# The memory's rows split in the attention, and the mixers' four 8 KB slots kept through the cross attention

## The chip, the cores and the metric

The kernel runs on one core of a Trainium2 chip. The metric is device microseconds of one execution, the median of several runs. Every row of a trace below comes from one execution that the hardware profiler recorded.

## What is computed

One decoder layer on a sequence of 512 tokens of width 1024, in four sub-layers with residual adds, each behind an RMS norm: half a SwiGLU feed-forward layer (inner width 2816), two parallel mixers (a spatial gating unit and a causal dilated window attention), a cross attention of four heads to 256 fixed memory rows, and another half feed-forward layer. What the change touches lies in the second and third:

```python
y_a = chunked_spatial_gating(z_sgu, sgu_ln_g[l], sgu_ln_b[l], sgu_w_s[l], sgu_b_s[l])
y_b = dilated_mixture_attention(q, k, v).reshape(b, s, D_ATT)
y = jnp.concatenate([rmsnorm(y_a, out_norm_a[l]), rmsnorm(y_b, out_norm_b[l])], axis=-1)
x = x + y @ w_out[l]

h = rmsnorm(x, cross_norm[l])
m = rmsnorm(mem, mem_norm[l])
x = x + memory_cross_attention(h, m, cross_wq[l], cross_wk[l], cross_wv[l], cross_wo[l])
```

## The kernel before

Everything is kept transposed, as eight tiles `X[d]` of 128 channels by 512 tokens in SBUF. Every product is made as three matmuls of a shortened format: each operand is split into a high part and a low part (`split`, L103 on ScalarE for the high part and L104 on VectorE for the low part, the source less the high part), and `mm3` (L127 to L129) adds high x high, high x low and low x high in PSUM. In the trace L129 is the matmul that needs a weight's low part, `wlo`, and L127 and L128 need `whi` only.

Weights pass through `load_weight` (L116): a raw tile `wraw` by DMA from SyncE's queue (SP), then the split into `whi` and `wlo`. The raw, high and low tiles have three slots each, so the weights of a fourth matrix tile are split when the first one's matmuls are done.

PSUM has four banks for long sums (`acc`) and four for short ones (`aux`).

The kernel is written against a framework with a planner. It orders each engine's instructions ahead of time, by their place in the program and a cost model, lets a later instruction go first when an earlier one isn't ready by the model, gives out the slots of a pool's tag in that order and sets the semaphores. On the chip each engine then works through its own list in that order.

The stages around the change, in the order of the program:

- `mixers`: a pool `mix` holds U, V and the normalised V as high and low part (`vnH`, `vnL`), four tiles of 8 KB per partition under the tag `t8`. `z_block` makes the five blocks of the input projection. Then come 32 units of the window attention, (m, r, i) for four head pairs, two heads and four tiles of 128 queries: `scores(u)` makes the score row and its softmax, `transposes(u - 3)` turns the probabilities, `values(u - 4)` multiplies them with v and writes `yH`, `yL` for inner tile 4 + m. `qk_transpose(1)`, ahead of unit 12, turns the q and k of the second two head pairs out of the tiles `qk` and splits them (`qkH`, `qkL`).
- At the end of `mixers` the sum of squares of the attention's output becomes `Rb`: `Stats.column` (L186), eleven short VectorE steps (`rsqrt_cols`, L134 to L143), `dg` (L151), one matmul (L153), one copy (`R`, L157).
- `cross` opens a pool of its own where `mix` lay, and calls `mem_split` first. It loads the memory's 1024 x 256 values in four transfers of two tiles (`mraw`, L664, two slots), scales each tile by its gain and the memory's norm (L666), and splits them into `mH`, `mL`, in eight slots of the pool of 512-wide tiles `hp`.
- `mix_out` is the output projection. Part 0 takes the four inner tiles of the gating unit, part 1 the four of the attention, each for d = 0 to 7 with twelve matmuls. Part 0 adds its sum to X (L627). Part 1 multiplies it with `Rb` (`yo`, L630), adds it to X (L631), and splits X for the next norm (`hH` L202, `hL` L203), with its square (L178), which GpSimd adds up (L170).
- Then the value projection of the memory (`xvH`, `xvL`, four tiles of 4 KB), the key projection, the queries, scores and values of four heads with `xpt` (four slots of 4 KB), and the output projection.

Of the kernel before, what the change touches and what calls it, by code (L numbers as in the profile page):

```python
# [17 lines left out]
F32 = mybir.dt.float32  # L18
F32R = mybir.dt.float32r
I32 = mybir.dt.int32  # L20
AF = mybir.ActivationFunctionType
ALU = mybir.AluOpType
AX = mybir.AxisListType

P = 128
S = 512
D = 1024
KD = D // P
# [4 lines left out]
NM = 256  # L33
NT = S // P
# [12 lines left out]
G_FFN1, G_MIX, G_CROSS, G_MEM, G_FFN2, G_FIN, G_OA, G_OB, G_BS = (  # L47
    0, 8, 16, 24, 32, 40, 48, 52, 56)
# [6 lines left out]
def body(tc, I, out):  # L55
    nc = tc.nc
    from contextlib import ExitStack
    ctx = ExitStack()
    with ctx:
# [27 lines left out]
        def gcol(off, k):  # L87
            return gains[:, off + k:off + k + 1]
# [4 lines left out]
        def aux_tile():  # L93
            return paux.tile([P, S], F32, name="aux", tag="aux")

        def h_tile(n):
            return hp.tile([P, S], F32R, name=n, tag="h")

        def f32(ap):
            return ap.bitcast(F32)  # L100

        def split(hi, lo, src):
            ins = nc.scalar.activation(hi, src, AF.Copy)  # L103
            nc.vector.tensor_sub(lo, src, f32(hi))  # L104
            return ins
# [280 lines left out]
        def h_sl(h, k, ts):  # L386
            return h[0][k][:, ts], h[1][k][:, ts]

        def mixers(norm, cs):
            col = []  # L390
            hshape = [P, 8, 64]
            with tc.tile_pool(name="mix", bufs=1) as mp:
# [12 lines left out]
                split(ws[0], ws[1], wsr)  # L405


                U = mp.tile([P, NT, S], F32, name="U", tag="t8", bufs=4)
                V = mp.tile([P, NT, S], F32, name="V", tag="t8", bufs=4)

                def gelu_to(dst):
                    def evac(t, acc):
                        nc.scalar.activation(dst[:, t], acc, AF.Gelu, scale=col[0][:, t:t + 1])
                    return evac

                z_block(norm, 0, gelu_to(U), lambda: col.append(norm.stats.column(D)))
                z_block(norm, 1, gelu_to(V))

                qk = {}
# [18 lines left out]
                def qk_transpose(b):  # L438
                    for m in range(4):
                        ps = aux_tile()  # L440
                        for t in range(NT):
                            nc.tensor.transpose(ps[:, t * P:(t + 1) * P],
                                                qk[t][:, m * P:(m + 1) * P], ident_b)
                        if m >= 2:
                            hi, lo = h_tile("qkH"), h_tile("qkL")
                            split(hi, lo, ps)
                            kT[2 * b + m % 2] = (hi, lo)
                            continue


                        qT[2 * b + m % 2] = []
                        for r in range(2):
                            hi, lo = h_tile("qkH"), h_tile("qkL")
                            rows, other = (slice(x * 64, (x + 1) * 64) for x in (r, 1 - r))
                            for x in (hi, lo):
                                nc.gpsimd.memset(f32(x[other]), 0.0)
                            split(hi[rows], lo[rows], ps[rows])
                            qT[2 * b + m % 2].append((hi, lo))

                vH = [h_tile("vH") for _ in range(NT)]  # L460
                vL = [h_tile("vL") for _ in range(NT)]

                def v_evac(t, acc):
# [9 lines left out]

                mu = mp.tile([P, NT, 8], F32, name="mu")
                var = mp.tile([P, NT, 8], F32, name="var")
                vn = (mp.tile([P, NT, S], F32R, name="vnH", tag="t8", bufs=4),
                      mp.tile([P, NT, S], F32R, name="vnL", tag="t8", bufs=4))
                for t in range(NT):
                    vt = V[:, t].rearrange("p (g c) -> p g c", g=8)
                    nc.vector.tensor_reduce(mu[:, t], vt, axis=AX.X, op=ALU.add)  # L480
                    nc.vector.tensor_scalar(mu[:, t], mu[:, t], 1.0 / 64, None, op0=ALU.mult)
                    nc.vector.tensor_sub(vt, vt, mu[:, t, :, None].to_broadcast(hshape))
                    sq = mp.tile([P, S], F32, name="vsq", tag="s2", bufs=SB)
                    nc.scalar.activation(sq, V[:, t], AF.Square)
                    nc.vector.tensor_reduce(var[:, t], sq.rearrange("p (g c) -> p g c", g=8),
                                            axis=AX.X, op=ALU.add)
                rs = rsqrt_cols(var.rearrange("p t g -> p (t g)"), NT * 8, 1.0 / 64, LN_EPS, "lnr")
                for t in range(NT):
                    vt = V[:, t].rearrange("p (g c) -> p g c", g=8)
                    r = rs[:, t * 8:(t + 1) * 8]  # L490
                    nc.vector.tensor_mul(vt, vt, r[:, :, None].to_broadcast(hshape))
                    nc.vector.tensor_mul(V[:, t], V[:, t], lng)
                    nc.vector.tensor_add(V[:, t], V[:, t], lnb)
                    split(vn[0][:, t], vn[1][:, t], V[:, t])
# [72 lines left out]
                def gate_mix():  # L567

                    for g in range(0, 8, 2):
                        ps = aux_tile().rearrange("p (a t c) -> p a t c", a=2, t=NT)  # L570
                        for a in range(2):
                            cs_ = slice((g + a) * 64, (g + a + 1) * 64)
                            mm3(ps[:, a], ws, (vn[0][:, :, cs_], vn[1][:, :, cs_]),
                                (slice(None), g + a), slice(None), True, True)
                            nc.vector.scalar_tensor_tensor(U[:, :, cs_], ps[:, a],
                                                           gcol(G_BS, g + a), U[:, :, cs_],
                                                           op0=ALU.add, op1=ALU.mult)
                    ssa = mp.tile([P, NT], F32, name="ssa")
                    for t in range(NT):
                        sq = mp.tile([P, S], F32, name="usq", tag="s2", bufs=SB)  # L580
                        nc.scalar.activation(sq, U[:, t], AF.Square, accum_out=ssa[:, t:t + 1])
                    ra = rsqrt_cols(ssa, NT, 1.0 / S, NORM_EPS, "ra4")
                    for t in range(NT):
                        nc.scalar.activation(U[:, t], U[:, t], AF.Copy, scale=ra[:, t:t + 1])

                yH, yL = [None] * KD, [None] * KD

                def gate_out():
                    for b in range(4):
                        ps = aux_tile()  # L590
                        for t in range(NT):
                            nc.tensor.transpose(ps[:, t * P:(t + 1) * P],
                                                U[:, t, b * P:(b + 1) * P], ident)
                        yH[b], yL[b] = h_tile("yH"), h_tile("yL")
# [5 lines left out]
                nu = len(units)  # L600
# [5 lines left out]
                for u in range(LAG, nu + LAG + 1):  # L606
                    if u == nu // 2 - LAG - 1:
                        qk_transpose(1)
                    if u < nu:
                        scores(u)  # L610
                    transposes(u - LAG) if u - LAG < nu else None
                    if u > LAG:
                        values(u - LAG - 1)
# [20 lines left out]
        mem = {}  # L634
# [22 lines left out]
            elif step == 4:  # L657
                mem["R"] = rows(mem["col"], 2, "mR")

        def mem_split(pool, mR):  # L660
            mH, mL = [], []
            for k in range(0, KD, 2):
                raw = pool.tile([P, 2, NM], F32, name="mraw", tag="mraw", bufs=2)
                nc.sync.dma_start(raw, I["memT"][k:k + 2].rearrange("k p n -> p k n"))  # L664
                for j in range(2):
                    nc.vector.scalar_tensor_tensor(raw[:, j], raw[:, j], gcol(G_MEM, k + j), mR,  # L666
                                                   op0=ALU.mult, op1=ALU.mult)
                hi = h_tile("mH").rearrange("p (k n) -> p k n", k=2)
                lo = h_tile("mL").rearrange("p (k n) -> p k n", k=2)
                split(hi, lo, raw)  # L670
                mH += [hi[:, 0], hi[:, 1]]
                mL += [lo[:, 0], lo[:, 1]]
            return mH, mL

        def cross(norm, y, mR, nxt):
            with tc.tile_pool(name="cross", bufs=1) as cp:
                m = mem_split(cp, mR)
                mix_out(cp, *y, norm)

                vH = [cp.tile([P, D], F32R, name=f"xvH{t}") for t in range(2)]  # L680
                vL = [cp.tile([P, D], F32R, name=f"xvL{t}") for t in range(2)]
                for blk in range(2):
                    acc = [acc_tile() for _ in range(2)]
                    for kk in range(4):
                        w = load_weight(I["wv"][blk, kk], [2, S])
                        for t in range(2):
                            for k2 in range(2):
                                k = 2 * kk + k2
# [73 lines left out]
                for h in range(4):  # L762
                    scores(h, 0)
                    scores(h, 2)
                    if h < 3:
                        queries(2 * h + 2)
                    pt = tuple(cp.tile([P, 2, S], F32R, name="xpt", tag="xpt", bufs=4)
                               for _ in range(2))
                    transposes(h, 0, pt)
                    transposes(h, 2, pt)  # L770
                    if h < 3:
                        queries(2 * h + 3)
                    values(2 * h, pt)
                    values(2 * h + 1, pt)
# [15 lines left out]
        n1, n2, n3, n4 = (  # L790
            Norm(g, t) for g, t in ((G_FFN1, 1), (G_MIX, 0), (G_CROSS, 0), (G_FFN2, 0)))
# [6 lines left out]
        cs = []  # L798
# [5 lines left out]
                mem_rows(d)  # L804

        ffn(n1, I["gate1"], I["up1"], I["down1"], n2, lambda: w0, between)
        y = mixers(n2, cs[0])
        cross(n3, y, mem["R"], n4)
        ffn(n4, I["gate2"], I["up2"], I["down2"], None)


# [83 lines left out]
```

## Time and profile before

| | |
|---|---|
| median of three runs | 1129.87 us (1128.18 to 1129.97) |
| the profiled execution | 1129.09 us |
| its span | 1127.3 us |
| TensorE busy | 1110.1 us (98%) |
| VectorE busy | 590.9 us (52%) |
| ScalarE busy | 425.0 us (38%) |
| GpSimd busy | 74.3 us (7%) |

The span is the time from the first to the last instruction in the trace; the execution's own time lies 1.8 us above it. Shares of busy time are means over stages that differ much. Matmuls are pipelined, so that their durations overlap: how far apart two of them start says more than how long one is.

### The profile page before, as it was taken

The numbers are of one execution on the slowest core, as the hardware profiler recorded it, in microseconds if no ns is written. First come the engines' busy times: TensorE is split into PE (matmuls) and PEld (weight loads), VectorE is DVE, ScalarE is ACT, GpSimd is POOL, SyncE is SP. The second block draws the span as 40 slices with busy tenths as digits, with TensorE's granted clock in tenths as the row PEclk, the third lists the DMA queues.
The fourth block names the chain that finished last, engine by engine and source line by source line (L and its number), as shares of the span: only waits on it lengthen the run. The fifth ranks groups of instructions, "written<-read, shape, count | busy, mean of one in ns | idle before, by whom it ended". The sixth has DMA issues, their size and how long they took to land. (4 is left out here: it accounts for less than half of the span.)

```text
span 1127.3 us, 13958 instructions
## 1 busy us (share of the span) xinstructions
PE 1110.1 (98%) x5472; PEld 934.7 (83%) x5472; DVE 590.9 (52%) x1027; ACT 425.0 (38%) x672; POOL 74.3 (7%) x98
## 2 busy tenths in 40 slices
PE   9999999999999999999989999999999999999996
PEld 7788888888888888888868988878888888888996
DVE  4544533444444447679796555455444334445542
ACT  6333312233233434568665344333332222333421
POOL 2000100000002200011121000120000000000011
PEclk9999999999999999999999999999999999999998
DMA  6322334222233423110136421222222333223511
GB/s 220 113 94 89 115 89 126 105 94 94 72 92 109 149 90 108 38 48 29 57 118 203 147 75 57 72 97 90 98 93 66 103 113 111 95 94 115 155 64 38
DMA packets 39698, 110.79 MB, mean 98 GB/s; under 512 B 4432, under 2 KB 9296, under 8 KB 39632
## 3 DMA queue, kind: packets, MB, share of 16 engines
q1 hardware_dynamic: 39632, 109.89, 30.3%
q8 instruction: 43, 0.70, 0.2%
q14 instruction: 23, 0.19, 0.1%
HBM read 107.78 MB, written 2.10 MB: 97 GB/s over the span
## 5 line engine op out<-in xcount | busy, mean ns | idle before, releaser
L103 ACT ACTIVATE whi<-wraw 128x1024 fp32r<-128x1024 f32 (+2 forms) x213 | 202.8, 953 | 513.9 <-PE acc L128 298.6
L104 DVE TENSOR_TENSOR wlo<-wraw,whi 128x1024 fp32r<-128x1024 f32 (+2 forms) x213 | 237.0, 1115 | 163.0 <-ACT whi L103 162.7
L127 PE MATMUL acc<-hH,whi 128*128 128x512 f32 x768 | 301.0, 392 | 0.6 <-ACT hH L202 0.6
L128 PE MATMUL acc<-hL,whi 128*128 128x512 f32 x768 | 299.4, 390 | 0.8 <-DVE hL L203 0.8
L129 PE MATMUL acc<-hH,wlo 128*128 128x512 f32 x768 | 299.4, 390 | 0.5 <-DVE wlo L104 0.5
L128 PEld LDWEIGHTS acc<-hL,whi 128*128 128x128 f32 x768 | 144.3, 188 | 31.5 <-DVE hL L203 1.5
L127 PEld LDWEIGHTS acc<-hH,whi 128*128 128x128 f32 x768 | 144.3, 188 | 31.4 <-ACT hH L202 1.0
L129 PEld LDWEIGHTS acc<-hH,wlo 128*128 128x128 f32 x768 | 144.3, 188 | 30.7 <-DVE wlo L104 1.0
L127 PE MATMUL acc<-hidH,whi 128*128 128x512 f32 (+1 forms) x308 | 115.6, 375 | 0.0
L129 PE MATMUL acc<-hidH,wlo 128*128 128x512 f32 (+1 forms) x308 | 115.3, 374 | 0.0
L128 PE MATMUL acc<-hidL,whi 128*128 128x512 f32 (+1 forms) x308 | 115.3, 374 | 0.0
L170 POOL TENSOR_TENSOR sq<-sq 128x512 f32<-128x512 f32 (+1 forms) x39 | 49.2, 1260 | 775.5 <-ACT sq L178 775.1
L247 DVE TENSOR_TENSOR u<-acc,R 128x512 f32<-128x512 f32 x44 | 30.4, 690 | 121.6 <-PE acc L129 121.6
L243 DVE TENSOR_TENSOR gp<-acc,R 128x512 f32<-128x512 f32 x44 | 30.4, 691 | 85.4 <-PE acc L129 81.7
L129 PEld LDWEIGHTS acc<-hidH,wlo 128*128 128x128 f32 x308 | 58.1, 189 | 10.3
L128 PEld LDWEIGHTS acc<-hidL,whi 128*128 128x128 f32 x308 | 58.1, 188 | 10.3
L127 PEld LDWEIGHTS acc<-hidH,whi 128*128 128x128 f32 x308 | 58.1, 189 | 10.2
L127 PE MATMUL acc<-whi,hH 128*128 128x512 f32 x160 | 62.5, 391 | 0.0
L129 PE MATMUL acc<-whi,hL 128*128 128x512 f32 x160 | 62.4, 390 | 0.0
L230 DVE SCALAR_TENSOR_TENSOR x<-acc,x 128x512 f32<-128x512 f32 (+1 forms) x40 | 23.3, 584 | 74.6 <-PE acc L129 74.6
L128 PE MATMUL acc<-wlo,hH 128*128 128x512 f32 x160 | 62.3, 390 | 0.0
L178 ACT ACTIVATE sq<-x 128x512 f32<-128x512 f32 (+1 forms) x48 | 26.1, 551 | 41.5 <-DVE x L230 38.9
(213 smaller groups left out, 1488.1 us busy)
## 6 DMA issues: line engine op xcount, KB each, us to landing
wraw<-up SPq DMA_DIRECT2D x44, 512.0 KB, 3.5
wraw<-gate SPq DMA_DIRECT2D x43, 512.0 KB, 3.5
wraw<-down SPq DMA_DIRECT2D x28, 384.0 KB, 3.1
wraw<-w_in SPq DMA_DIRECT2D x20, 512.0 KB, 3.5
wraw<-down SPq DMA_DIRECT2D x28, 320.0 KB, 2.9
wraw<-w_out SPq DMA_DIRECT2D x16, 256.0 KB, 2.7
wraw<-wv SPq DMA_DIRECT2D x8, 512.0 KB, 3.5
wraw<-wk SPq DMA_DIRECT2D x8, 512.0 KB, 4.2
```

What stands on the lines that cost most here:

```text
L103: ins = nc.scalar.activation(hi, src, AF.Copy)
L104: nc.vector.tensor_sub(lo, src, f32(hi))
L127: nc.tensor.matmul(ps, lhsT=aH, rhs=bH, start=start, stop=False)
L128: nc.tensor.matmul(ps, lhsT=aH, rhs=bL, start=False, stop=False)
L129: nc.tensor.matmul(ps, lhsT=aL, rhs=bH, start=False, stop=stop)
L170: nc.gpsimd.tensor_add(self.parts[0], self.parts[0], sq)
L178: nc.scalar.activation(sq, src, AF.Square)
L230: nc.vector.scalar_tensor_tensor(X[d][:, tok], acc, 0.5, X[d][:, tok], op0=ALU.mult, op1=ALU.add)
L243: nc.vector.tensor_mul(gp, ps[0], R)
L247: nc.vector.tensor_mul(u, ps[1], R)
```

## The change

A pool `big` with the four 8 KB slots of tag `t8` is opened around `mixers` and `cross`. U, V, `vnH`, `vnL` are taken from it as before. `mem_split` moves into the loop of the attention, ahead of unit 16 of 32; its four raw tiles take the four slots of `qk` in the mixers' pool (they had two slots of their own), and its results are two tiles of 8 KB in `big`, not eight of `hp`. In `cross` the memory's values `xvH`, `xvL` become two 8 KB tiles of `big`, and the high and low part of a head's probabilities, `xpt`, share one 8 KB tile of `big`. What is computed stays the same, instruction by instruction.

```diff
-        def mixers(norm, cs):
+        def mem_split(pool, big, mR):
+            mH, mL = (big.tile([P, KD, NM], F32R, name=n, tag="t8", bufs=4) for n in ("mH", "mL"))
+            for k in range(0, KD, 2):
+                raw = pool.tile([P, 2, NM], F32, name="mraw", tag="qk", bufs=4)
+                nc.sync.dma_start(raw, I["memT"][k:k + 2].rearrange("k p n -> p k n"))
+                for j in range(2):
+                    nc.vector.scalar_tensor_tensor(raw[:, j], raw[:, j], gcol(G_MEM, k + j), mR,
+                                                   op0=ALU.mult, op1=ALU.mult)
+                split(mH[:, k:k + 2], mL[:, k:k + 2], raw)
+            return [mH[:, k] for k in range(KD)], [mL[:, k] for k in range(KD)]
+
+        def mixers(norm, cs, big):
...
-                U = mp.tile([P, NT, S], F32, name="U", tag="t8", bufs=4)
-                V = mp.tile([P, NT, S], F32, name="V", tag="t8", bufs=4)
+                U = big.tile([P, NT, S], F32, name="U", tag="t8", bufs=4)
+                V = big.tile([P, NT, S], F32, name="V", tag="t8", bufs=4)
...
                 for u in range(LAG, nu + LAG + 1):
                     if u == nu // 2 - LAG - 1:
                         qk_transpose(1)
+                    if u == nu // 2:
+                        mem["split"] = mem_split(mp, big, mem["R"])
                     if u < nu:
                         scores(u)
...
-        def cross(norm, y, mR, nxt):
+        def cross(norm, y, m, nxt, big):
             with tc.tile_pool(name="cross", bufs=1) as cp:
-                m = mem_split(cp, mR)
                 mix_out(cp, *y, norm)
 
-                vH = [cp.tile([P, D], F32R, name=f"xvH{t}") for t in range(2)]
-                vL = [cp.tile([P, D], F32R, name=f"xvL{t}") for t in range(2)]
+                vH, vL = (big.tile([P, 2, D], F32R, name=n, tag="t8", bufs=4)
+                          for n in ("xvH", "xvL"))
+                vH, vL = ([x[:, t] for t in range(2)] for x in (vH, vL))
...
-                    pt = tuple(cp.tile([P, 2, S], F32R, name="xpt", tag="xpt", bufs=4)
-                               for _ in range(2))
+                    pt = big.tile([P, 2, 2, S], F32R, name="xpt", tag="t8", bufs=4)
+                    pt = tuple(pt[:, i] for i in range(2))
...
-        y = mixers(n2, cs[0])
-        cross(n3, y, mem["R"], n4)
+        with tc.tile_pool(name="big", bufs=1) as big:
+            y = mixers(n2, cs[0], big)
+            cross(n3, y, mem["split"], n4, big)
```

## Rows read from the trace of the kernel before

**Rows 1.** The page's first two parts: busy microseconds of each engine with its share of the span and its instructions; then the span in 40 equal slices of 28 us, a digit being the busy share in tenths.

```profile
PE 1110.1 (98%) x5472; PEld 934.7 (83%) x5472; DVE 590.9 (52%) x1027; ACT 425.0 (38%) x672; POOL 74.3 (7%) x98
...
DVE  4544533444444447679796555455444334445542
```

**Rows 2.** Busy time of each engine by windows of time (from the span's start): the window's length, then busy microseconds and instructions of each engine, then the mean granted clock of TensorE, the busy share of the DMA engines and GB/s.

```profile
510.00:520.00 10.00, 9.95 (x63) 8.24 (x62) 9.63 (x28) 8.61 (x22) 0.48 (x2) 1.00 0.01 2
520.00:530.00 10.00, 10.00 (x68) 8.74 (x66) 9.37 (x32) 7.58 (x22) 1.16 (x6) 1.00 0.16 47
530.00:540.00 10.00, 10.00 (x67) 8.87 (x66) 8.85 (x31) 8.07 (x24) 2.34 (x7) 1.00 0.18 61
540.00:550.00 10.00, 10.00 (x63) 8.25 (x62) 9.57 (x31) 7.90 (x22) 2.01 (x5) 1.00 0.07 27
...
555.00:560.00 5.00, 5.00 (x33) 4.33 (x32) 2.88 (x5) 2.09 (x5) 0.00 (x0) 1.00 0.20 57
...
575.00:580.00 5.00, 1.18 (x5) 0.42 (x4) 5.00 (x7) 2.31 (x4) 2.05 (x2) 1.00 0.00 0
580.00:590.00 10.00, 10.00 (x37) 8.06 (x38) 9.96 (x12) 5.51 (x7) 4.71 (x3) 0.83 0.58 210
```

**Rows 3.** TensorE's matmuls of part 1 of `mix_out` in order of time: start and duration in us, engine, line, output and inputs, and in brackets the idle time before and what ended it.

```profile
558.66 0.40 PE L127 MATMUL acc<-yH,whi 128*128 128x512 f32 x1
...
574.28 0.39 PE L127 MATMUL acc<-yH,whi 128*128 128x512 f32 x1
...
574.96 0.39 PE L128 MATMUL acc<-yL,whi 128*128 128x512 f32 x1
577.09 0.47 PE L127 MATMUL acc<-yH,whi 128*128 128x512 f32 x1 [1.74 <-DVE yo L630]
...
579.88 0.50 PE L129 MATMUL acc<-yH,wlo 128*128 128x512 f32 x1 [2.09 <-DVE wlo L104]
...
581.03 0.63 PE L127 MATMUL acc<-yH,whi 128*128 128x512 f32 x1
581.45 0.63 PE L128 MATMUL acc<-yL,whi 128*128 128x512 f32 x1
...
584.01 0.47 PE L127 MATMUL acc<-yH,whi 128*128 128x512 f32 x1
584.33 0.40 PE L128 MATMUL acc<-yL,whi 128*128 128x512 f32 x1
```

**Rows 4.** Windows again, of two microseconds behind that wait; the third number from the end is the granted clock.

```profile
582.00:584.00 2.00, 2.00 (x6) 1.53 (x5) 2.00 (x5) 1.79 (x3) 0.40 (x1) 0.50 0.31 125
```

**Rows 5.** VectorE in order of time from the rsqrt for `Rb` to the `wlo` that TensorE waits for.

```profile
561.19 0.16 DVE L134 TENSOR_SCALAR rcolbv<-aux 128x4 f32<-128x4 f32 x1 [1.33 <-PE aux L186]
...
562.19 0.16 DVE L141 TENSOR_TENSOR rcolbt<-rcolby 128x4 f32<-128x4 f32 x1
...
565.48 0.87 DVE L151 TENSOR_SCALAR dg<-const,rcolby 128x128 f32<-128x128 f32 x4
...
567.51 0.88 DVE L666 SCALAR_TENSOR_TENSOR mraw<-mraw,gains,R 128x256 f32<-128x256 f32 x2
568.30 0.69 DVE L630 TENSOR_TENSOR yo<-acc,R 128x512 f32<-128x512 f32 x1
568.90 0.48 DVE L666 SCALAR_TENSOR_TENSOR mraw<-mraw,gains,R 128x256 f32<-128x256 f32 x1
569.30 0.68 DVE L104 TENSOR_TENSOR mL<-mraw,mH 128x512 fp32r<-128x512 f32 x1
569.90 0.48 DVE L666 SCALAR_TENSOR_TENSOR mraw<-mraw,gains,R 128x256 f32<-128x256 f32 x1
...
574.56 1.77 DVE L203 SCALAR_TENSOR_TENSOR hL<-x,gains,hH 128x512 fp32r<-128x512 f32 x1
...
579.15 0.68 DVE L104 TENSOR_TENSOR wlo<-wraw,whi 128x512 fp32r<-128x512 f32 x1
```

**Rows 6.** ScalarE and GpSimd in order of time around the same place, and a GpSimd add in the attention.

```profile
567.63 0.60 ACT L157 ACTIVATE R<-aux 128x512 f32<-128x512 f32 x1 [2.04 <-PE aux L153]
...
568.96 0.62 ACT L103 ACTIVATE whi<-wraw 128x512 fp32r<-128x512 f32 x1
...
530.12 1.28 POOL L170 TENSOR_TENSOR sqb<-sqb 128x512 f32<-128x512 f32 x1 [1.78 <-ACT sqb L563]
...
573.58 2.21 POOL L170 TENSOR_TENSOR sq<-sq 128x512 f32<-128x512 f32 x1 [21.55 <-ACT sq L178]
```

**Rows 7.** The instructions that touch the memory's tiles, and the `hL` of 560 to 600 us: durations in ns (min/median/max), first and last start in us; the last row is the time from issue to landing of the memory's transfers in us (min/median/max).

```profile
L103 ACT ACTIVATE mH<-mraw x4: 632/632/635, 563.4 to 570.4; 128x512 fp32r<-128x512 f32 x4
...
DMA to landing us min/median/max: 2.6/3.6/4.6
...
L203 DVE SCALAR_TENSOR_TENSOR hL<-x,gains,hH x8: 736/742/1774, 573.3 to 595.5; 128x512 fp32r<-128x512 f32 x8
```

**Rows 8.** What TensorE waited for in 460 to 560 us, the whole list: in total, times, longest, in us.

```profile
PE aux L127 <- DVE yL L597: 0.2, 1, 0.2
```

**Rows 9.** What SP's queue waited for in 500 to 600 us, its longest entry: in total, times, longest, in us.

```profile
SPq L116 <- DVE wlo L104: 89.6, 18, 15.3
```

**Rows 10.** VectorE in order of time at the splitting of the second q and k.

```profile
511.65 2.75 DVE L104 TENSOR_TENSOR qkL<-aux,qkH 128x512 fp32r<-128x512 f32 x4 [0.17 <-ACT qkH L103]
514.31 0.28 DVE L512 CUSTOM_DVE_ANT_0 s<-aux,const 128x128 f32<-128x128 f32 x1
```

More of the change, by code (lines that the diff above doesn't have):

```diff
@@ L475, in mixers @@
                 var = mp.tile([P, NT, 8], F32, name="var")
-                vn = (mp.tile([P, NT, S], F32R, name="vnH", tag="t8", bufs=4),
-                      mp.tile([P, NT, S], F32R, name="vnL", tag="t8", bufs=4))
+                vn = (big.tile([P, NT, S], F32R, name="vnH", tag="t8", bufs=4),
+                      big.tile([P, NT, S], F32R, name="vnL", tag="t8", bufs=4))
                 for t in range(NT):
@@ L658, in mem_rows @@
                 mem["R"] = rows(mem["col"], 2, "mR")
[L660 to L673, printed above, removed]
-        def cross(norm, y, mR, nxt):
+        def cross(norm, y, m, nxt, big):
             with tc.tile_pool(name="cross", bufs=1) as cp:
-                m = mem_split(cp, mR)
                 mix_out(cp, *y, norm)
-                vH = [cp.tile([P, D], F32R, name=f"xvH{t}") for t in range(2)]
-                vL = [cp.tile([P, D], F32R, name=f"xvL{t}") for t in range(2)]
+                vH, vL = (big.tile([P, 2, D], F32R, name=n, tag="t8", bufs=4)
+                          for n in ("xvH", "xvL"))
+                vH, vL = ([x[:, t] for t in range(2)] for x in (vH, vL))
                 for blk in range(2):
```

## The prediction

> **What bounds the kernel now.** I read the page's first two parts first: TensorE is busy for 98% of the span, so at most the other 2% can be had anywhere outside its own work, and the per-slice line shows VectorE nearly full only in the slices of the attention and of the output projection that follows it [rows 1]. Then the windows by stage around those slices, to see which engine runs out of slack first. In the attention TensorE is busy without a break and VectorE for 9.4 to 9.6 of 10 us; in 575 to 580 us TensorE is busy for 1.18 of 5 us while VectorE has no free time at all, and the next ten microseconds run at a mean granted clock of 0.83 [rows 2]. Last the instructions themselves at that spot. TensorE stands 1.74 us for the evacuation `yo` and 2.09 us for a `wlo`, and then its matmuls start 0.43 us apart where they were 0.23 apart before [rows 3]; the granted clock there is 0.50, the lower level of 1.2 GHz [rows 4].
>
> I price the hole as a whole. From 574.96 to 584.33 us 15 matmuls start (574.96 is the first, 584.01 the last). At 0.227 us each, the spacing from 574.28 to 574.96, they would take 3.4 us; they take 9.4. **The hole is worth 6.0 us**, 3.8 of it waiting and the rest the clock after it and the restarts. Nothing else near the change is as large: in 460 to 560 us TensorE waits 0.2 us in all [rows 8].
>
> Why the hole is there: `wlo` of the sixth output tile of part 1 (d=5) starts on VectorE at 579.15 [rows 5], though its `whi` started on ScalarE at 568.96 [rows 6]. In between VectorE works without a break through the evacuations of the first tiles, and through half of `mem_split`. The other half of `mem_split` stands among the eleven short steps of the rsqrt for `Rb` and holds up `dg`, and with it R, and with R the first evacuation [rows 5].
>
> **What the change removes here.** The rsqrt starts at 561.19 and goes in steps of 0.20 us (561.19 to 562.19 are five); eleven take 2.2 us, so `dg` could start at 563.4 and not at 565.48: R comes 2.1 us earlier. Then between 568.90 and 572.10 two scalings (0.40 each, start to start) and two subtractions (0.60 each, 569.30 to 569.90) stand in the evacuation queue: 2.0 us. So 4.1 us of delay leave VectorE's queue here; the two scalings at 567.51 lie in the wait for R and give nothing. ScalarE loses four copies of 0.63 us [rows 7], which costs and gives nothing, since it waits 2 us before R in any case [rows 6].
>
> **What it adds in the attention.** The same work: eight scalings at 0.40 and four subtractions at 0.60 are 5.6 us of VectorE; four copies of 0.63 are 2.5 us of ScalarE; four issues on SP's queue. The raw tiles take the slots of `qk`, which the last transposes of q and k leave, and the split takes two of the four 8 KB slots that U, V and vn have left by then. The code puts it ahead of unit 16, so it comes in about 514 to 530 us. VectorE's free time in those two windows is 0.37 + 0.63 = 1.0 us [rows 2]. **The attention's end therefore moves by 5.6 - 1.0 = 4.6 us.** Bounds: 3.0 us, if all of the 2.6 us that VectorE is free from 510 to 550 took some of it [rows 2], and 5.6 us, if none did. I take the upper part, since the nearest row is the splitting of the transposed q and k, 2.75 us of VectorE from 511.65, and nothing of it was absorbed: the next score row stands behind it, at 514.31 [rows 10]. What the wait queues: behind the scalings on VectorE stand the score rows, the probability splits and the `wlo` of the output projection; the matmuls of unit 13 and later wait for those. On SP the four loads stand ahead of one or more loads of w_out.
>
> *Does TensorE stand for 4.6 us?* No, if its order gives it other work. It has the rest of part 0 of `mix_out`, which now ends just before the attention does, and, behind that, the first three inner tiles of part 1 for d = 0 to 2, for which the attention's first three head pairs suffice: 27 matmuls x 0.227 = 6.1 us, of which nothing runs before 558.66 now [rows 3]. But d = 1 and 2 need their `wlo` for that, 2 x 0.6 us of VectorE that now come ahead of the attention's end: **1.2 us, which I put on TensorE.** Bounds: 0 (the qk splitting costs TensorE no wait now [rows 8]) and 4.6 (no filler is placed).
>
> **A rule weighed.** Some VectorE operations in the hole take far longer than their kind: `hL` 1.77 us where its median is 0.74, as GpSimd adds squares from 573.58 for 2.21 us [rows 5, 6, 7]. The Trainium skill, "SBUF — State Buffer", section "Who interferes with whom", says that a VectorE instruction with two inputs in SBUF is fully blocked by a GpSimd instruction that reads SBUF, and not by one that only writes it. The rows agree. By the rule the moved subtractions and scalings would be free of this beside the attention's memsets, and pay up to 1.3 us if they met the add of 530.12 us; going by it the sum below would be 0 to 1.3 us worse.
>
> **After the attention.** It ends at about 558.5 + 4.6 = 563.1. Of d = 0 to 2 only nine matmuls (2.0 us) are left, so their weight slots are free by 566 and `whi`, `wlo` of d = 3 to 5 (ScalarE 0.63, VectorE 0.6 each) are done by 569, in the time in which VectorE waits for R. R comes at 567.63 - 2.1 + 4.6 = 570.1, its copy takes 0.6, and `yo` starts at 570.8. So the `wlo` that now opens the hole is out of the queue. What is late next is `wlo` of d = 6: its slot comes free only when d = 3 is done, so it stands behind the evacuations. From the first `yo` to that place is 579.15 - 568.30 = 10.85 us now, less the 2.0 of `mem_split`: 8.85. It starts at 579.65 and ends at 580.3. TensorE would want it: d = 4 ends at 574.28 [rows 3], d = 5 at 577.0, and four matmuls that need no `wlo` run ahead (0.9): 577.9. **A hole of 2.4 us stays.** Bounds: 0 (VectorE's order puts it earlier) and 6.0 (the present hole).
>
> **Sum.** -6.0 + 2.4 + 1.2 = **-2.4 us**. The profiled execution took 1129.09 us, 1127.3 of it the span; the median of the runs is 0.78 above it. From 1129.09 it is 1126.7, from the median, which I forecast against, **1127.5 us**. The rest has one answer and costs nothing: xv and the probabilities of the cross attention take 8 KB slots that are free before they are asked for (V and vn are last read ahead of the attention, the memory's rows by the last key matmul), two heads deep as before; eight h tiles come free; the pool opens and closes at the same two places of the program. Its cover is TensorE's unbroken stream in the value and key projections.
>
> **Rivals.**
> *The hole goes wholly* (chance 0.10): the order puts `wlo` ahead of the evacuations, 2.4 becomes 0. -6.0 + 1.2 = -4.8: 1125.1 us. For it: 4.1 us less in that queue. Against: the evacuations stand ahead of weights today.
> *VectorE gives it all back* (0.30): the filler isn't drawn forward, so `wlo` of d = 5 stays where it is; it ends at 579.8 - 4.1 + 4.6, 0.5 us later than now. +0.5: 1130.4 us. Work is only moved from one full stretch of VectorE to another, and the free time that `mem_split` filled while R was made is lost. For it: 9.4 to 9.6 us of 10 [rows 2]. Against: VectorE is free for 2.1 us of the window at 555 [rows 2], which then can hold weights.
> *VectorE stands for the memory's rows* (0.22, the slower side): the loads go through SP's queue, which waits up to 15.3 us at a stretch for a `wlo` of VectorE [rows 9]; if they are issued late, VectorE stands in order at the first scaling with the whole attention behind it. One landing is 3.6 us [rows 7]; with 5.6 us of work that is 9.2 us that TensorE can't cover with 6.1 us of filler unless the order has it there; if none is, -6.0 + 9.2 = +3.2: 1133.1 us. It decides when the waiting in the attention exceeds the 6.0 us of the hole. Against: the slots are free from about 512 us, and transfers are few there.
> That the change doesn't do what it says I leave out: loads and splits have no other place to go.
>
> **How the numbers follow.** Forecast 0.38 with its own range 1126.2 to 1128.6; the others as above. 0.2% is 2.26 us, about what a measurement of this kernel can tell from no change, so the borders are 1127.6 and 1132.1. Faster: 0.32 of the forecast and the 0.10 of the first rival, 0.42. Same: 0.06 of the forecast, 0.28 of the second, 0.02 of the third, 0.36. Slower: 0.22. The range reaches from below the first rival (1124.2) to just under the third's price (1132.6), and leaves out about half of the third and a little of the first.
>
> **What would show it.** Right: the eight scalings lie between 512 and 535 us; the rsqrt runs through in 2.2 us; the attention ends 4 to 5 us later in TensorE's own work; matmuls of part 1 stand before its end; the wait for `wlo` near 578 is at most 2.5 us and the clock stays up. Wrong: a wait of TensorE above 2 us between 510 and 565, a wait of VectorE for the memory's load, or a clock of 0.5 after the attention. The sum fails first where I know least: whether the order places the filler.

## The result and the profile after

The changed kernel takes **1131.86 us** (median of 22 runs, 1130.44 to 1132.82); the kernel before takes 1129.84 in as many. The ratio is 1.0016 (95% interval 1.0009 to 1.0023), so the change makes it slower by 2.0 us. The forecast was 1127.5 us. The profiled execution took 1132.03 us, its span 1130.3. The granted clock of TensorE differs between the 22 runs: 7 with a mean of 0.997 took 1130.44 to 1131.38 us, the other 15 (0.994 to 0.996, the profiled one at 0.994 among them) 1131.25 to 1132.82, so not every run loses to the clock what the trace below shows.

The windows of the changed kernel by stage, to set beside [rows 2] (same columns):

```profile
510.00:520.00 10.00, 9.94 (x63) 8.20 (x62) 9.60 (x28) 8.66 (x22) 0.42 (x2) 1.00 0.35 107
520.00:530.00 10.00, 7.92 (x41) 6.26 (x39) 9.68 (x28) 6.58 (x17) 0.77 (x4) 0.84 0.00 1
530.00:540.00 10.00, 9.24 (x59) 7.38 (x59) 9.21 (x32) 7.62 (x22) 2.49 (x7) 0.99 0.00 0
540.00:550.00 10.00, 9.82 (x64) 8.12 (x63) 9.21 (x33) 8.28 (x23) 1.03 (x6) 1.00 0.24 81
...
570.00:580.00 10.00, 10.00 (x45) 8.20 (x44) 8.63 (x12) 5.77 (x10) 1.38 (x1) 1.00 0.34 107
580.00:590.00 10.00, 10.00 (x46) 8.29 (x45) 9.96 (x11) 6.81 (x11) 5.60 (x4) 1.00 0.38 111
590.00:600.00 10.00, 8.85 (x37) 6.37 (x36) 9.59 (x11) 5.03 (x7) 3.66 (x3) 1.00 0.46 155
```

TensorE runs through 570 to 590 us at the full clock: the hole is gone. But in 520 to 530 us it starts 41 matmuls where it started 68 [rows 2], at a mean granted clock of 0.84, and VectorE is as full as before. A smaller loss stands at 590 to 600.

VectorE in order of time, at the place where the split now stands:

```profile
504.13 0.68 DVE L104 TENSOR_TENSOR wlo<-wraw,whi 128x512 fp32r<-128x512 f32 x1
...
519.61 0.47 DVE L395 SCALAR_TENSOR_TENSOR mraw<-mraw,gains,R 128x256 f32<-128x256 f32 x1
...
521.37 0.69 DVE L104 TENSOR_TENSOR mL<-mraw,mH 128x512 fp32r<-128x512 f32 x1
521.98 1.27 DVE L395 SCALAR_TENSOR_TENSOR mraw<-mraw,gains,R 128x256 f32<-128x256 f32 x3
...
525.00 0.48 DVE L395 SCALAR_TENSOR_TENSOR mraw<-mraw,gains,R 128x256 f32<-128x256 f32 x1
525.39 0.28 DVE L523 CUSTOM_DVE_ANT_0 s<-aux,const 128x128 f32<-128x128 f32 x1
...
526.28 0.69 DVE L104 TENSOR_TENSOR mL<-mraw,mH 128x512 fp32r<-128x512 f32 x1
...
539.26 0.68 DVE L104 TENSOR_TENSOR wlo<-wraw,whi 128x512 fp32r<-128x512 f32 x1
```

The low parts that the kernel before made in that time:

```profile
519.76 0.68 DVE L104 TENSOR_TENSOR wlo<-wraw,whi 128x512 fp32r<-128x512 f32 x1
...
527.37 0.68 DVE L104 TENSOR_TENSOR wlo<-wraw,whi 128x512 fp32r<-128x512 f32 x1
528.04 0.67 DVE L104 TENSOR_TENSOR wlo<-wraw,whi 128x512 fp32r<-128x512 f32 x1
...
535.94 0.66 DVE L104 TENSOR_TENSOR wlo<-wraw,whi 128x512 fp32r<-128x512 f32 x1
```

And TensorE's matmuls in the changed kernel, and the window from 528 to 530 us, columns as above:

```profile
523.26 0.40 PE L128 MATMUL acc<-yL,whi 128*128 128x512 f32 x1
525.74 0.39 PE L127 MATMUL aux<-pt,vH 128*128 128x256 f32 x1 [2.08 <-DVE nmx L523]
...
529.34 0.63 PE L129 MATMUL aux<-qkH,qkL 128*128 128x512 f32 x1
```
```profile
528.00:530.00 2.00, 2.00 (x9) 1.37 (x7) 1.85 (x5) 0.98 (x2) 0.00 (x0) 0.50 0.00 0
```

The split goes in front of the evacuation of a score row (L523, at 525.39), and TensorE stands 2.1 us for that bank. Then a 512-wide matmul takes 0.63 us, as it did behind the old hole [rows 3, 4], and the granted clock is 0.50: the lower of the two clock levels. The first and the last row of VectorE are the larger matter. No low part of a weight is made between 504.13 and 539.26 us, where the kernel before made four. It isn't the weights that are late: ScalarE makes `whi` at 506.67, 514.04 and 522.21 us (506.64, 514.00 and 522.54 before), and the first of the three low parts starts 32 us after its `whi` is done. Without the low parts the matmuls of the output projection that fill TensorE's gaps can't run: 35 of them start from 520 to 557.5 us, where 52 did.

Both losses show in one count: the instructions on the projection's sums (`acc`) from 510 us to the start of the rsqrt, before and changed (TensorE's matmuls stand in the first bracket, then weight loads, VectorE, ScalarE; clock and DMA as in [rows 2]):

```profile
510.00:561.19 51.19, 24.16 (x78) 13.36 (x79) 4.07 (x6) 0.00 (x0) 1.00 0.12 38
```
```profile
510.00:564.99 54.99, 20.38 (x67) 11.46 (x68) 3.39 (x5) 0.00 (x0) 0.97 0.15 49
```

The attention ends 3.8 us later, and by then 11 matmuls fewer have started, 2.5 us at their undisturbed spacing: 6.3 us, close to the 6.0 of the table below.

**Lost time** below is a stretch's elapsed time between its first and last matmul start, less what its matmuls take at the spacing that they have undisturbed in this kernel (0.2275 us for 512 columns, 0.171 for 384, 0.1165 for 256, 0.113 for a 128-wide transpose). It counts waits and clock together, a wait where it begins. Read differences between rows: the 2.2 us of the kernel before in the attention are no wait [rows 8] but what matmuls of other widths and kinds take beyond these spacings, and by how those are priced the differences move by up to 0.5 us. Worked out from the starts in the traces, in us:

| kernel | median | ratio to before (95%) | 510 to 570 | 570 to 590 | 590 to 600 |
|---|---|---|---|---|---|
| before | 1129.84 | | 2.2 | 6.0 | 0.0 |
| changed | 1131.86 | 1.0016 (1.0009 to 1.0023) | 8.2 | 0.0 | 2.0 |
| e1 slots only | 1133.07 | 1.0031 (1.0020 to 1.0043) | 2.1 | 9.8 | 0.0 |
| e2 late | 1132.61 | 1.0024 (1.0014 to 1.0033) | 8.8 | 0.0 | 2.0 |
| e3 early | 1126.06 | 0.9967 (0.9955 to 0.9980) | 1.9 | 2.4 | 0.0 |
| e4 spread | 1133.48 | 1.0033 (1.0021 to 1.0045) | 9.6 | 0.0 | 1.3 |
| e5 no scaling | 1129.27 | 0.9996 (0.9987 to 1.0005) | 4.5 | 0.8 | 2.2 |
| e6 early, extra | 1133.50 | 1.0035 (1.0023 to 1.0048) | 9.1 | 0.0 | 2.4 |
| e7 before, ahead | 1134.84 | 1.0044 (1.0032 to 1.0057) | 1.7 | 10.3 | 2.4 |
| e8 early, ahead | 1126.66 | 0.9974 (0.9963 to 0.9985) | 1.7 | 2.3 | 1.0 |
| e9 early, no adds | 1123.26 | 0.9947 (0.9933 to 0.9960) | 1.9 | 0.0 | 0.0 |
| e10 early, adds on VectorE | 1127.87 | 0.9984 (0.9975 to 0.9993) | 1.8 | 3.2 | 1.4 |
| e11 early, in PSUM | 1124.99 | 0.9959 (0.9947 to 0.9972) | 1.7 | 1.4 | 0.1 |
| e12 changed, in PSUM | 1129.43 | 0.9993 (0.9984 to 1.0002) | 7.8 | 0.0 | 0.0 |

The changed kernel's row is the answer in short: -6.0 at the hole, +6.0 in the attention, +2.0 at 590.

### The profile page after: what moved, and what is told of

Read it like the earlier page. It is cut to its first block, busy times and chain, and to the rows that moved or that the text cites. A ratio compares the mean times of both kernels' runs of the same rounds, so it can differ in the third digit from the quotient of the medians.

```text
span 1130.3 us, 13961 instructions
## 1 busy us (share of the span) xinstructions
PE 1113.1 (98%) x5472; PEld 934.5 (83%) x5472; DVE 592.8 (52%) x1027; ACT 424.6 (38%) x672; POOL 74.8 (7%) x98
## 5 line engine op out<-in xcount | busy, mean ns | idle before, releaser
L127 PEld LDWEIGHTS acc<-hidH,whi 128*128 128x128 f32 x308 | 58.0, 188 | 10.3
L129 PEld LDWEIGHTS acc<-hidH,wlo 128*128 128x128 f32 x308 | 58.0, 188 | 10.3
L128 PEld LDWEIGHTS acc<-hidL,whi 128*128 128x128 f32 x308 | 58.0, 188 | 10.3
```

The lines of the kernel that those rows point to most:

```text
L127: nc.tensor.matmul(ps, lhsT=aH, rhs=bH, start=start, stop=False)
L128: nc.tensor.matmul(ps, lhsT=aH, rhs=bL, start=False, stop=False)
L129: nc.tensor.matmul(ps, lhsT=aL, rhs=bH, start=False, stop=stop)
```

## The experiments

Three theories stood at first. **A**: the split is one block ahead of unit 16, and it is the block that starves TensorE. **B**: VectorE is full in the attention, so that the same work costs the same anywhere in it. **C**: the exchanged slots cost something by themselves.

**e1, slots only.** The split goes back to the start of the cross attention; only the slots are the changed kernel's.

```diff
-                    if u == nu // 2:
-                        mem["split"] = mem_split(mp, big, mem["R"])
...
             with tc.tile_pool(name="cross", bufs=1) as cp:
+                m = mem_split(cp, big, mem["R"])
```

> Only the slots of the change are kept: the four 8 KB slots span the cross attention, and the memory's rows are split where the kernel before splits them, at the start of the cross attention (raw tiles in two slots of their own). Theory A (the split in one block ahead of unit 16 starves TensorE of evacuated banks and of low weight parts, 6.1 us in 520 to 550) and theory B (VectorE is full in the attention, any place in it costs as much): the hole of 6.0 us at 575 to 584 is back and nothing is lost in the attention, 1129 to 1130.5 us. Theory C (the exchanged slots themselves cost): 1131 us or more, with lost time behind the attention.

1133.07 us, 3.4 slower than before, outside the range of A and B. C gave 1131 us or more with the loss behind the attention, and so far it has this. But the attention loses nothing, and neither does anything behind 590 us; what has grown is the old hole. TensorE's wait:

```profile
575.63 0.40 PE L128 MATMUL acc<-yL,whi 128*128 128x512 f32 x1
583.26 0.79 PE L129 MATMUL acc<-yH,wlo 128*128 128x512 f32 x1 [7.23 <-DVE wlo L104]
```

The same `wlo` starts at 581.46 instead of 579.15 [rows 5]: the planner has put one more `hL` and one more add to X ahead of it, and it takes 1.75 us itself, where it took 0.68. With other slots the planner made another order of the same VectorE work, and a worse one. Why it did, no run shows. e3 below has the same slots and is faster than the kernel before, so a fixed price of the slots (C) falls.

**e2, late** and **e4, spread.** The split is called behind the last unit (e2), or one transfer of it ahead of each of the units 16, 20, 24, 28 (e4; `mem_pair` is one turn of the loop in `mem_split`).

```diff
+                mem["split"] = mem_split(mp, big, mem["R"])
                 Rb = rows(stats.column(S, "rcolb"))
```
```diff
-                    if u == nu // 2:
-                        mem["split"] = mem_split(mp, big, mem["R"])
+                    if u in (16, 20, 24, 28):
...
+                        mem_pair(mp, *mt, 2 * (16, 20, 24, 28).index(u), mem["R"])
```

> The split is called behind the last unit of the attention, still in the mixers' pool, so that it comes after all units in the order of the program and can only take VectorE's free moments from about 512 us on. A: the block is broken up, TensorE loses under 2 us in 510 to 560 and the hole behind the attention is 0 to 3 us: 1126 to 1129 us. B: VectorE has 2.6 us free from 510 to 550, so half or more of the 5.6 us still push the attention or stay behind it: 1130 to 1132 us. C: as after, 1131 us or more.

> One of the four transfers with its two scalings and its split ahead of each of the units 16, 20, 24 and 28: the same work in the attention, in four pieces of 1.4 us. A: TensorE's banks and weights outlast 1.4 us, it loses under 3 us in 510 to 560: 1127 to 1130 us. B: the attention ends as late as with the block and TensorE loses 5 to 6 us in it: 1131 to 1132.5 us.

1132.61 and 1133.48 us: A falls, and both lie above what B gave, by 0.6 and 1.0 us. The windows of e2 from 520 to 560 us:

```profile
520.00:530.00 10.00, 8.82 (x60) 7.52 (x59) 9.53 (x34) 9.22 (x25) 1.05 (x6) 1.00 0.00 1
530.00:540.00 10.00, 8.46 (x56) 7.02 (x56) 9.82 (x33) 7.84 (x22) 2.36 (x7) 1.00 0.00 0
540.00:550.00 10.00, 8.44 (x54) 6.80 (x55) 9.94 (x34) 7.90 (x21) 1.96 (x5) 1.00 0.01 2
550.00:560.00 10.00, 9.27 (x62) 8.06 (x61) 7.40 (x17) 4.58 (x12) 0.39 (x2) 1.00 0.25 79
```

No wait above 1.1 us, no slow clock, and still 6.6 us more lost than before, in small pieces. In e2 the attention itself isn't late: its rsqrt starts at 559.02, where it started at 561.19 [rows 5]. What is late is part 0 of the output projection: from 520 to 557.5 us 18 of its matmuls start, in e4 14, in the kernel before 52. The split stands behind the units but ahead of the projection's weights in the order of the program, so the weights are what it pushes out: no `wlo` starts in e2 between 503.67 and 552.51 us. By the count above, e2's rsqrt is 2.2 us early, but 39 matmuls fewer have started by then, 8.9 us of work: 6.7 us net.

**e3, early.** The split is called behind the gating unit, ahead of the last block of the input projection.

```diff
                 gate_mix()
+                mem["split"] = mem_split(mp, big, mem["R"])
                 for u in range(LAG):
```

> The split is called behind the gating unit, ahead of the last block of the input projection, where TensorE runs 96 matmuls that need nothing of VectorE but a weight's low part, and VectorE is free for 5.3 of 20 us (480 to 500). A and B: nothing is lost in the attention, the hole of 6.0 us behind it goes, up to 2 us stay at 590 to 600 as in the changed kernel: 1125 to 1127 us. C: 1129 us or more.

1126.06 us. The memory's instructions of e3 from 440 to 600 us (ns, then first and last start), and the end of what is left of the hole:

```profile
L395 DVE SCALAR_TENSOR_TENSOR mraw<-mraw,gains,R x8: 474/476/484, 464.6 to 474.5; 128x256 f32<-128x256 f32 x8
...
L104 DVE TENSOR_TENSOR mL<-mraw,mH x4: 681/684/693, 472.3 to 477.8; 128x512 fp32r<-128x512 f32 x4
```
```profile
575.98 0.50 PE L129 MATMUL acc<-yH,wlo 128*128 128x512 f32 x1 [1.32 <-DVE wlo L104]
```

The planner runs the split still earlier than I thought, in 464 to 478 us, where TensorE is fed by the input projection. Nothing is lost in the attention, and `wlo` of d = 5 starts at 575.25, 3.9 us earlier than in [rows 5]. So the same work costs 6 us in one place and nothing in another 50 us ahead of it.

**e5, no scaling.** The changed kernel without the eight scalings; gain and norm of the memory are left out.

```diff
-                for j in range(2):
-                    nc.vector.scalar_tensor_tensor(raw[:, j], raw[:, j], gcol(G_MEM, k + j), mR,
-                                                   op0=ALU.mult, op1=ALU.mult)
```

> The changed kernel without the eight scalings of the memory's rows (the rows are split as they are loaded, gain and norm are left out): 3.2 us less of VectorE ahead of unit 16, the same four loads, four ScalarE copies and four subtractions. Theory B (VectorE is full in the attention, each microsecond put into it is lost to TensorE, since it is the low weight parts of the filler that wait): the 6.1 us lost in 520 to 550 fall in proportion, to 2.4 to 2.9, and the time to 1127.5 to 1129.5 us. Rival (the loads, their wait, or ScalarE's copies hold up the attention): 1131 us or more.

1129.27 us. With the loads, the copies on ScalarE and the subtractions all in place, 3.2 us less of VectorE take the loss in 510 to 570 from 6.0 above before to 2.3.

**e6, early and extra.** e3, with nine subtractions on VectorE that serve nothing.

```diff
+                    if u == nu // 2:
+                        extra = mp.tile([P, S], F32, name="extra", tag="qk", bufs=4)
+                        mask = const[:, C_MASK:C_MASK + S]
+                        for _ in range(9):
+                            nc.vector.tensor_sub(extra, mask, mask)
```

> The kernel with the early split, and ahead of unit 16 nine subtractions of 128x512 on VectorE into a tile that nobody reads (5.4 us of VectorE, no load, nothing on ScalarE). B: TensorE loses 5.5 to 7 us in 515 to 560 again, by VectorE alone, and part 0 of the output projection ends later: 1131 to 1133 us. Rival (loads or ScalarE): TensorE loses under 2 us there, 1126 to 1128 us.

1133.50 us, 0.5 above the range given. Its windows:

```profile
520.00:530.00 10.00, 8.03 (x47) 5.96 (x45) 9.58 (x25) 5.51 (x15) 0.77 (x4) 0.95 0.01 2
530.00:540.00 10.00, 9.59 (x47) 8.31 (x48) 8.49 (x28) 6.36 (x18) 2.04 (x5) 0.71 0.07 26
```

5.4 us of VectorE alone cost 7.2 us against e3 in 510 to 570, with the same thinning of matmuls and the same fall of the clock. The loads and ScalarE aren't needed for it. B stands.

**e7 and e8, weights ahead.** The projection asks for the weights of tile n + 3 ahead of tile n's evacuation, in the kernel before and in e3.

```diff
+            todo = [(part, d) for part in range(2) for d in range(KD)]
+            ws = [load_weight(I["w_out"][i], [4, P]) for i in todo[:3]]
...
+                    if n + 3 < len(todo):
+                        ws.append(load_weight(I["w_out"][todo[n + 3]], [4, P]))
```

> The kernel before, but the output projection asks for the weights of tile n + 3 right behind the matmuls of tile n and ahead of tile n's evacuation, so that the low part comes first in VectorE's order. If the hole of 6.0 us is one of order (the low part stands behind evacuations that nobody waits for): it shrinks to 0 to 3 us, 1124 to 1127 us. If it is one of VectorE's total in that stretch: 1129 us or more, as the same work stays.

> Both: the early split and the weights asked for ahead of the evacuation. The early split left 2.4 us at 575 to 580, of which 1.9 are waits for low parts. Order theory: these go too, 1123 to 1125 us. Total theory: 1126 us, as with the early split alone.

1134.84 and 1126.66 us: that the hole is one of order falls. In e7 the weights of w_out are in time, and the evacuations that they passed stand in front of the next weights, those of the value projection:

```profile
PE acc L128 <- DVE wlo L104: 9.0, 1, 9.0
```

The hole moved from 575 to 583 us and grew. In the kernel before VectorE works almost without a break from `yo` at 568.30 [rows 5] to 596.2 us, while TensorE stands for 6 us of that time: VectorE has more to do there than TensorE. The order says where that shows and, since e1 and e7 lose more with the same work, also how much of it; which order loses least, no run shows.

**e9, e10, e11: what makes VectorE slow there.** e3 with GpSimd's seven adds of squares left out (the third norm then rests on one square of eight), with the adds on VectorE (`nc.vector.tensor_add` in their place), and with the product with `Rb` made in place in PSUM.

```diff
-                    nc.gpsimd.tensor_add(self.parts[0], self.parts[0], sq)
+                    if self.how == "pool":
+                        nc.gpsimd.tensor_add(self.parts[0], self.parts[0], sq)
...
+        n3.stats.how = "none"
```
```diff
-                        t = pool.tile([P, S], F32, name="yo", tag="yo", bufs=2)
-                        nc.vector.tensor_mul(t, acc, Rb)
-                        nc.vector.tensor_add(X[d], X[d], t)
+                        nc.vector.tensor_mul(acc, acc, Rb)
+                        nc.vector.tensor_add(X[d], acc, X[d])
```

> The early split, without GpSimd's seven adds of squares behind part 1 (the third norm then rests on the first square alone; the other sums are left out). Theory: VectorE's total between 566 and 600 us bounds that stretch, and its operations with two inputs in SBUF stand still while GpSimd reads: six of them are 0.5 to 1.1 us longer than their kind, 4.7 us in all. Without the adds hL is 0.74 and x 0.68 throughout, the 2.4 us left at 575 to 580 go: 1123 to 1124.5 us. Rival (GpSimd's adds are beside the point): 1126 us.

> The early split, with those seven adds on VectorE, 0.6 us each, 4.2 us, in place of GpSimd. Theory: VectorE wins 4.7 us of standing still and pays 4.2: 1125.5 to 1126.5 us, no change that can be told from the early split. Rival (GpSimd doesn't matter): 4.2 us more of VectorE, 1129 us or more.

> The early split, and part 1 of the output projection multiplies its sum with Rb in place in PSUM, so that the add to X has only one input in SBUF. Theory: the adds to X are 0.67 to 0.69 us throughout (they were up to 1.77 beside GpSimd's add), VectorE wins some 2 us, the bank comes free 0.6 us later: 1124 to 1126 us. Rival (bank time decides): 1127 us or more.

1123.26, 1127.87 and 1124.99 us. Groups of VectorE from 556 to 600 us, busy us and mean ns: first e3, then e9, then e11.

```profile
L643 DVE TENSOR_TENSOR x<-x,yo 128x512 f32<-128x512 f32 x8 | 7.6, 955 | 0.0
L203 DVE SCALAR_TENSOR_TENSOR hL<-x,gains,hH 128x512 fp32r<-128x512 f32 x8 | 7.4, 929 | 0.1
```
```profile
L205 DVE SCALAR_TENSOR_TENSOR hL<-x,gains,hH 128x512 fp32r<-128x512 f32 x8 | 6.0, 744 | 0.1
L645 DVE TENSOR_TENSOR x<-x,yo 128x512 f32<-128x512 f32 x8 | 5.4, 684 | 0.0
```
```profile
L203 DVE SCALAR_TENSOR_TENSOR hL<-x,gains,hH 128x512 fp32r<-128x512 f32 x8 | 8.2, 1026 | 0.4 <-ACT hH L202 0.2
...
L642 DVE TENSOR_TENSOR x<-acc,x 128x512 f32<-128x512 f32 x8 | 5.4, 681 | 0.0
```

Without the adds the means are those of undisturbed instructions (744 and 684 ns) and the hole is gone. With one input in PSUM the adds to X are short though GpSimd still adds; part of the standing still moves to `hL` (929 to 1026 ns), and about 1 us is won; the intervals of e3 and e11 overlap, but e12 below wins 2.4 us by the same edit. The adds on VectorE (e10) cost 1.8 us net against e3, 1.4 above the range: I had put 4.2 of work against 4.7 of standing still. **e11 beats both kernels**, by 4.5 us against the one before in its own runs.

**e12, changed and in PSUM.** The last diff on the changed kernel.

> The changed kernel with the product with Rb made in place in PSUM, as in the run before. Theory: the 2.0 us that the changed kernel loses at 590 to 600 us are the rest of the hole, VectorE being late there since its adds to X stand still beside GpSimd; they fall below 1 us, the 6.1 us in the attention stay: 1130 to 1131 us. Rival (the loss at 590 has another cause, such as the loads of wv): no change, 1131.5 to 1132.5 us.

1129.43 us, 0.6 below the range: the 2.0 us at 590 go, and the 5.6 us in the attention stay.

## Why the prediction was wrong

- *The hole, 6.0 us, and its cause.* Right in size, and right that a `wlo` stands behind VectorE's queue. The relief of 4.1 us is 3.9 in e3. How long the hole is hangs on the planner's order as well (e1).
- *The attention's end moves by 4.6 us.* It moved by 3.8 (the rsqrt starts at 564.99, not 561.19 [rows 5]). The rsqrt then took 3.1 us instead of 2.2, since the last add of part 0 and a weight's low part had got in among its steps, so that `yo` starts at 570.98 where 570.8 was forecast: two errors that cancel.
- ***"Does TensorE stand for 4.6 us? No ... 1.2 us, which I put on TensorE."* This step failed.** TensorE lost 6.0 us there. I charged the filler with the two low parts of d = 1 and 2 alone and took the rest (27 matmuls, 6.1 us) to be drawn forward. Every tile of filler needs VectorE: a low part and an add to X, 1.2 us for 2.7 us of matmuls, and they stand behind the units in the program. With VectorE full, work put ahead of them pushes the filler back: the last add of part 0 came at 566.06 us, not 557.56, behind the end of the attention instead of ahead of it, and 93 of the projection's 192 matmuls had started at the rsqrt instead of 104, where the forecast had more than 104. So the bound that I named, "no filler is placed", 4.6 us, was too low: it kept the filler that ran there already, and that was pushed out too. The sign of being wrong that I gave, a wait above 2 us between 510 and 565, came (2.08). Of VectorE's work in the attention a microsecond cost TensorE 1.0 to 1.3: 6.0 for 5.6 in the changed kernel, 6.6 and 7.4 in e2 and e4, 7.2 for 5.4 in e6, 2.3 for the 2.4 left in e5.
- *A hole of 2.4 us stays, for `wlo` of d = 6.* It was 0 there, and not because the order was better. VectorE's side of this term came true: `wlo` of d = 6 starts at 579.49 us (579.65 forecast). But TensorE, late by what it had lost in the attention, wants it only at about 583.7 (counted back from the end of part 1 at 588.48, twelve matmuls a tile), not at 577.9. The failed step hid this hole. Then 2.0 us were lost at 590 for the weights of the value projection, where VectorE was late for the same reason. That these 2.0 are near the 2.4 of the term is luck. I had said that this projection's stream covers what the rest costs; it has waits itself where VectorE is late.
- *The rest costs nothing.* Not settled: e1 is 3.4 us slower than before with the slots alone, through another order at the hole. In the changed kernel that hole doesn't exist, so the slots can't be charged for its 2.0 us.
- *The sum*, then: -6.0 + 6.0 + 2.0 = +2.0, measured 2.0 between the medians. Between the two traces, from which the terms come, it is 3.0 (spans 1130.3 and 1127.3), so that about 1 us lies in small pieces outside the three stretches, and the close agreement is partly luck.
- *The rivals.* "VectorE gives it all back" had the reason (work moved from one full stretch to another) and the wrong road (the old hole staying). "VectorE stands for the memory's rows" named +3.2, 1.2 us too much, and the wrong mechanism: from 510 to 530 us VectorE waits 0.2 us in all, and never for a load. (The landing of 3.6 us in its price is the median of all eight loads of the memory [rows 7]; the four in question took 2.6 to 3.1.)
- *The rule weighed.* The Trainium skill ("SBUF — State Buffer", "Who interferes with whom") says that a VectorE instruction with two inputs in SBUF contends with a GpSimd instruction that reads SBUF. e9 and e11 agree: a VectorE instruction with two inputs in SBUF stands while GpSimd reads (955 ns in the mean for 684), one with an input in PSUM doesn't (681). I used the rule to look at the moved instructions, which GpSimd left alone (scalings at most 0.48 us, subtractions 0.69), and not at the ones that stayed, where the blocking cost 1 to 3 us (e11 and e9 against e3, e12 against the changed kernel).

## What to carry to other kernels

That TensorE is at 100% in a stage says nothing of slack if another engine at 95% makes what TensorE fills its gaps with: ask what each filler instruction needs of the full engine, and where it stands in that engine's order. Work that is hoisted out of a hole belongs in a stage where its own engine has time (here 50 us earlier: from 460 to 480 us the kernel before has VectorE busy for 14.1 of 20 us), not in the next free place of the program. When putting one waiting item first only moves the hole (e7), look at the engine's total in the stretch; making its instructions shorter, as reading one operand from PSUM did here, helped in both orders tried (e11, e12).

## What the runs showed of the hardware

- Two-input VectorE instructions beside GpSimd's adds: 0.68 to 0.75 us alone, up to 1.79 beside one; in e9, without the adds, none of the eight adds to X is above 0.69 us.
- TensorE's granted clock fell to the lower level behind a single wait of 2.1 us in the changed kernel (0.50 from 528 to 530 us, matmuls of 0.63 us), and in e6 behind three waits of 0.36, 0.41 and 0.65 us between 526 and 529 us (0.50 from 529 to 535). It stayed at 1.00 through e2, where waits reached 1.1 us and the time lost in the attention is nearly that of e6 (8.8 and 9.1 us). In these three runs neither the longest wait nor the lost time alone told whether the clock holds.
